# A two-layer transformer trunk on one core: reciprocal roots in three steps, spread by four column products

## The chip, the core and the metric

The kernel runs on one core of a Trainium2 chip. The metric is the device time of one execution in microseconds (us). Before the change three runs gave 1095.64, 1095.83 and 1101.1 us, median 1095.83. The engines are named as in the profile: PE is TensorE (matrix products; PEld is its loading of the stationary operand), DVE is VectorE, ACT is ScalarE, POOL is GpSimd, and SP issues the DMA transfers.

## What is computed

The reference runs two layers over 512 tokens of 1024 channels. Layer 0 has attention (four global heads, four windowed heads, and 256 context tokens as extra keys), layer 1 a Fourier mixing with a linear map. Each layer ends with a gated feed-forward part of width 2816 with a depthwise convolution of three taps. Every sub-layer stands between two RMS norms:

```python
def rms_norm(x, g):
    xf = x.astype(F32)
    y = xf * lax.rsqrt(jnp.mean(xf * xf, axis=-1, keepdims=True) + EPS)
    return (y * g.astype(F32)).astype(x.dtype)
...
        x = x + g1 * rms_norm(y, norm_g[i, 1])
        h = modulate(rms_norm(x, norm_g[i, 2]), sh2, sc2)
        x = x + g2 * rms_norm(conv_ffn(h, ffn_w_up[i], ffn_conv_w[i], ffn_conv_b[i], ffn_w_down[i]), norm_g[i, 3])
```

So between any two large products there is a sum of squares over the 1024 channels, a reciprocal root for each token, and a multiplication of every channel of a token by that root.

## The kernel before

Channels lie on the 128 partitions in eight blocks, and the tokens along the free dimension, in two halves of 256 tokens. All large products are made as three products of split numbers (`mm3`, lines 107 to 110): a high part and a low part of each operand. The kernel is written with a scheduler that sets the order of the instructions on each engine from priorities (`later`), from dependences added by hand (`follow`, `in_turn`, `behind_pe`), and from its own estimate of when operands are ready. Each engine then runs its queue strictly in that order, so a place in PE's queue that is not yet ready holds up all products behind it.

A norm of 256 tokens goes through these steps:

- Sums: `stat_add` (line 211) multiplies the squares by a matrix of ones, a quarter of the tokens (64) at a time, into four strips of 32 partitions each. The sum of token quarter j stands on partitions 32j to 32j+31, in 64 columns.
- Root: `rstd` (lines 214 to 222) works on those 128x64 numbers. ACT makes a first value (line 217); DVE makes one Newton step in four instructions (lines 218 to 221), the first of which scales the sum and the others use ACT's value.
- Spread: `spread` (lines 240 to 251) brings all 256 roots to all partitions. DVE multiplies the 128x64 roots by a mask of 128x4 (line 242), which gives 128x256 numbers with only one partition in 32 kept per quarter; one product of 256 columns with a selecting matrix (line 247) sums over the partitions into PSUM; ACT copies the result to SBUF (line 250), unless `copy=False`.

`spread` is called 14 times: three times at the start (the `R` steps of `START`), four times around the first feed-forward part (`joined`, line 379), twice before the Fourier mixing (`gated`, line 419, and `spread_on`, line 429), twice at the way from the Fourier mixing into the second feed-forward part (`joint`, line 460, for token half 0 and half 1), twice in that part (lines 1559 and 1564), and once in `boundary` (line 370) near the end. In `joint` for half 0 there are also small products without use, `busy` (line 203), which keep PE running while it waits; the last two of them (line 471) read the masked roots. The spread of half 1 is tied behind an update of half 0 (`after=self.mark`, line 463).

The squares of an output block are added up by `YStat.add` (lines 296 to 321): POOL adds the blocks 1 to 6 into an accumulator (line 318), and the last block is summed on PE with the accumulator.

At the very end of the program (lines 1913 to 1921) the last norm does not use `rstd` and `spread`. `stat_all` (line 225) multiplies by a whole 128x128 matrix of ones, so that the sums of 256 tokens are at once on all partitions, and `rstd_all` (line 228) makes the root there on 128x256 numbers: two ACT and three DVE instructions. Then DVE multiplies and adds, two channel blocks at a time, and four DMAs write the output.

Of the kernel before, what the change touches and what calls it, by code (L numbers as in the profile page):

```python
# [19 lines left out]
P = 128  # L20
# [61 lines left out]
K_ID, K_SEL, K_QD, K_ALL = 0, 128, 256, 260  # L82
# [3 lines left out]
def kernel(ctx: ExitStack, tc: tile.TileContext, a):  # L86
# [116 lines left out]
    def busy(ps, src, n):  # L203
        for _ in range(n):
            PE.matmul(ps[:32, :src.shape[1]], lhsT=ones32, rhs=src, start=True, stop=True)
# [8 lines left out]
    def rstd(ps):  # L214
        w = ps.shape[1]
        v, t, r = (mk(cp, [P, W4], F32, "st_" + c, n)[:, :w] for c, n in (("v", 2), ("t", 1), ("r", 1)))
        S.activation(out=r, in_=ps, func=AF.Abs_reciprocal_sqrt, bias=eps, scale=1.0 / D)
        V.tensor_scalar(out=v, in0=ps, scalar1=1.0 / D, scalar2=EPS, op0=ALU.mult, op1=ALU.add)
        V.tensor_tensor(out=t, in0=r, in1=r, op=ALU.mult)
        V.scalar_tensor_tensor(out=t, in0=t, scalar=-0.5, in1=v, op0=ALU.mult, op1=ALU.mult)  # L220
        V.scalar_tensor_tensor(out=v, in0=t, scalar=1.5, in1=r, op0=ALU.add, op1=ALU.mult)
        return v


    def stat_all(ps, sq, first, last):
        PE.matmul(ps[:, :HT], lhsT=ones32[:, :1].to_broadcast([P, P]), rhs=sq, start=first, stop=last)

    def rstd_all(ps):
        ps = ps[:, :HT]
        r, t, v = (md() for _ in range(3))  # L230
        R = mk(cp, [P, HT], F32, "Rs", 3)
        S.activation(out=r, in_=ps, func=AF.Abs_reciprocal_sqrt, bias=eps, scale=1.0 / D)
        S.activation(out=v, in_=ps, func=AF.Identity, bias=eps, scale=1.0 / D)
        V.tensor_tensor(out=t, in0=r, in1=r, op=ALU.mult)
        V.scalar_tensor_tensor(out=t, in0=t, scalar=-0.5, in1=v, op0=ALU.mult, op1=ALU.mult)
        V.scalar_tensor_tensor(out=R, in0=t, scalar=1.5, in1=r, op0=ALU.add, op1=ALU.mult)
        return R


    def spread(r, pps, tag="misc", copy=True, after=None):  # L240
        Rs = mk(cp, [P, HT], F32, "Rs", 3)
        i = V.tensor_tensor(out=Rs.rearrange("p (j w) -> p j w", j=4), in0=r.unsqueeze(1).to_broadcast([P, 4, W4]),
                            in1=con[:, K_QD:K_QD + 4].unsqueeze(2).to_broadcast([P, 4, W4]), op=ALU.mult)
        if after is not None:
            follow(i, after)
        R = mk(pps, [P, T], F32, tag, 2)
        PE.matmul(R[:, :HT], lhsT=con[:, K_SEL:K_SEL + P], rhs=Rs, start=True, stop=True)
        if not copy:
            return R[:, :HT], Rs
        S.copy(out=Rs, in_=R[:, :HT])  # L250
        return Rs
# [33 lines left out]
    class YStat:  # L285

        def __init__(self, pool=None, direct=1, late=None):
            self.pool = pool
            self.late = late
            self.direct = direct  # L290
            self.acc = None
            self.n = [0, 0]
            self.ps = {}
            self.last = {0: [], 1: []}

        def add(self, pps, src, hs):
# [7 lines left out]
            if n == 0:  # L304
                S.activation(out=self.acc[:, sl], in_=src, func=AF.Square)
                return
            if self.late and hs == [1] and n >= KC - 3:
                sq = mk(self.late, [P, T], F32, "cv%d" % (n % 2), 2)
                S.activation(out=sq[:, sl], in_=src, func=AF.Square)
                self.last[1].append(sq)  # L310
                return
# [10 lines left out]

        def sums_all(self, pps, h):
            ps = mk(pps, [P, T], F32, "misc", 2)
            stat_all(ps, self.acc[:, halves[h]], True, False)
            stat_all(ps, self.last[h][0][:, halves[h]], False, True)
            return ps
# [89 lines left out]
    class Plain:  # L417
# [11 lines left out]
        def spread_on(self, r, pps):  # L429
            Rp, _ = spread(r, pps, copy=False)  # L430
            R = mk(cp, [P, HT], F32, "Rs", 3)
            S.copy(out=R, in_=Rp)
            self.h, self.R = 1, (Rp, R)
# [26 lines left out]
        def joint(self, ys, h, pps, am):  # L460
            hs = halves[h]
            if h:
                R = spread(rstd(ys.sums(pps, h)[:, :W4]), pps, after=self.mark)
            else:
                ps = ys.sums(pps, h)
                warm = mk(pps, [P, T], F32, "mm", 6)
                for s, n in zip(halves, HOT2):
                    busy(warm, ys.sq[:, s], n)
                with later(-10000):
                    R, Rs = spread(rstd(ps[:, :W4]), pps, copy=False)  # L470
                busy(warm, Rs, HOT2[2])
                self.ps = mk(pps, [P, T], F32, "mm", 6)
# [22 lines left out]
            else:  # L495
# [7 lines left out]
                self.mark = i[2][1]  # L503
# [915 lines left out]
    def ffn(l, xp, ready, pre, mid, gem, plain=None):  # L1419
        nonlocal xT  # L1420
        ys = YStat(late=xp.pool if l == 0 else None)
# [482 lines left out]
    with ExitStack() as es:  # L1904
# [11 lines left out]
        R = rstd_all(ys.sums_all(pps, 1))  # L1916
        for k in range(0, KC, 2):
            t = mk(cp, [P, T], F32, "sq", 2).rearrange("p (a b) -> p a b", a=2)
            V.tensor_tensor(out=t, in0=yT[:, k:k + 2, hb], in1=R.unsqueeze(1).to_broadcast([P, 2, HT]), op=ALU.mult)
# [4 lines left out]
def _constants():  # L1924
    con = np.zeros((P, K_ALL), np.float32)
    con[:, K_ID:K_ID + P] = np.eye(P)
    con[::32, K_SEL:K_SEL + P] = 1.0
# [88 lines left out]
```

## Time and profile before

| what | value |
|---|---|
| median of three runs | 1095.83 us |
| the profiled execution | 1097.22 us |
| its span, first to last instruction | 1095.4 us |
| time around the span | 1.8 us |
| PE busy, share of the span | 1068.3 us, 98% |
| DVE busy | 891.7 us, 81% |
| ACT busy | 600.4 us, 55% |
| POOL busy | 113.0 us, 10% |
| mean granted PE clock | 0.996 |

The profile has one row for each group of instructions of one line on one engine. A row of the timeline gives the start, the duration, the engine, the line, the operation, what it writes from what, the shape, the count and, in brackets, the idle time of the engine before it with the instruction that ended it. A row of the chain of waits gives the start, the time that the chain spent there, and the engine with the line. Products are pipelined: the start of one is where it enters, and its duration holds the way through the array, so the time that a product takes from others is read from start to start. The four-byte products that are not split (the spreads, the sums) appear as two records each, with a weight load for each record.

### The profile page before, as it was taken

To read this page: it belongs to the slowest core of one execution; us is meant where nothing else is said; L and a number is where in the kernel's file an instruction comes from. 1 tells how busy PE (TensorE), PEld (TensorE's weight loads), DVE (VectorE), ACT (ScalarE), POOL (GpSimd) and SP (SyncE) were. 2 spreads that over 40 slices of the span, in tenths; PEclk is the share of its full clock that TensorE was granted. 3 is DMA by queue.
4 is the path that set the end of the run, shared out by engine and by line. 5 is a ranking of instruction groups with operands and counts; after the bars stand their busy time and mean duration, and the time that the engine had idled before them with its cause. 6 is when DMAs were issued, how large, how long until landed. Compare 5 with 4: busy or idle time off the path is not lost.

```text
span 1095.4 us, 22485 instructions
## 1 busy us (share of the span) xinstructions
PE 1068.3 (98%) x9340; PEld 1008.1 (92%) x9340; DVE 891.7 (81%) x1450; ACT 600.4 (55%) x1055; POOL 113.0 (10%) x121
## 2 busy tenths in 40 slices
PE   9999999999999999999999999999999999999995
PEld 5699888879999999999999999979999999999995
DVE  5779877773679976978999777888997899889856
ACT  4442366675666633652465466767755465556533
POOL 0046122422100000000000010210000000000012
PEclk9999999999999999999999999999999999999998
DMA  9776100174231564336724610842205533322332
GB/s 367 283 259 212 39 3 37 65 275 162 78 155 39 174 250 163 146 101 246 255 92 150 233 53 21 254 131 117 96 30 161 206 106 115 113 90 99 118 143 78
DMA packets 33911, 156.53 MB, mean 143 GB/s; under 512 B 3472, under 2 KB 8208, under 8 KB 22160
## 3 DMA queue, kind: packets, MB, share of 16 engines
q1 hardware_dynamic: 32656, 150.89, 38.2%
q0 software_dynamic: 1152, 4.19, 1.7%
q8 instruction: 73, 1.20, 0.4%
q14 instruction: 30, 0.25, 0.1%
HBM read 148.78 MB, written 6.29 MB: 142 GB/s over the span
## 4 chain that ended last, share of the span: by engine, by line
PE 75%; DVE 13%; ACT 5%; DMA 4%; issue 2%; POOL 0%; DVEq 0%; POOLq 0%; SPq 0%; ACTq 0%
PE mm L108 20%; PE mm L110 20%; PE mm L109 20%; DVE wl L144 3%; PE PT L1112 1%; ACT wh L144 1%; PE gm L108 1%; DVE gacc L566 1%; DVE cv L1443 1%; DVE cv L1445 1%; PE gm L109 1%; PE gm L110 1%; ACT yT L365 1%; PE O L109 1%; PE S L108 1%
## 5 line engine op out<-in xcount | busy, mean ns | idle before, releaser
L144 ACT CAST wh<-raw 128x1024 fp32r<-128x1024 f32 (+2 forms) x206 | 190.0, 931 | 150.0 <-PE mm L109 103.2
L144 DVE TENSOR_TENSOR wl<-raw,wh 128x1024 fp32r<-128x1024 f32 (+2 forms) x206 | 220.2, 1075 | 24.9 <-ACT wh L144 24.8
L108 PE MATMUL mm<-hh,wh 128*128 128x256 f32 x856 | 238.7, 280 | 1.1 <-ACT sq L1381 0.8
L110 PE MATMUL mm<-hh,wl 128*128 128x256 f32 x856 | 237.5, 278 | 1.2 <-DVE wl L144 1.0
L109 PE MATMUL mm<-hl,wh 128*128 128x256 f32 x856 | 237.9, 278 | 0.4 <-DVE hl L368 0.3
L108 PEld LDWEIGHTS mm<-hh,wh 128*128 128x128 f32 x856 | 160.6, 188 | 3.4 <-ACT sq L1381 1.2
L110 PEld LDWEIGHTS mm<-hh,wl 128*128 128x128 f32 x856 | 160.6, 188 | 2.2 <-DVE wl L144 2.1
L109 PEld LDWEIGHTS mm<-hl,wh 128*128 128x128 f32 x856 | 161.5, 189 | 0.8 <-DVE hl L368 0.5
L108 PE MATMUL mm<-xh,wh 128*128 128x256 f32 x492 | 137.0, 279 | 0.0
L109 PE MATMUL mm<-xl,wh 128*128 128x256 f32 x492 | 136.7, 278 | 0.0
L110 PE MATMUL mm<-xh,wl 128*128 128x256 f32 x492 | 136.5, 278 | 0.0
L108 PE MATMUL mm<-zh,wh 128*128 128x256 f32 x384 | 107.1, 279 | 0.3
L109 PE MATMUL mm<-zl,wh 128*128 128x256 f32 x384 | 106.7, 278 | 0.0
L110 PE MATMUL mm<-zh,wl 128*128 128x256 f32 x384 | 106.7, 278 | 0.0
L108 PEld LDWEIGHTS mm<-xh,wh 128*128 128x128 f32 x492 | 92.4, 188 | 1.3 <-ACT yT L1472 0.4
L109 PEld LDWEIGHTS mm<-xl,wh 128*128 128x128 f32 x492 | 92.5, 188 | 0.6 <-issue 0.4
L110 PEld LDWEIGHTS mm<-xh,wl 128*128 128x128 f32 x492 | 92.4, 188 | 0.1
L108 PEld LDWEIGHTS mm<-zh,wh 128*128 128x128 f32 x384 | 72.2, 188 | 1.0 <-ACT sq L1379 0.9
L109 PEld LDWEIGHTS mm<-zl,wh 128*128 128x128 f32 x384 | 72.4, 189 | 0.0
L110 PEld LDWEIGHTS mm<-zh,wl 128*128 128x128 f32 x384 | 72.1, 188 | 0.0
L318 POOL TENSOR_TENSOR gacc<-gacc,sq 128x256 f32<-128x256 f32 (+1 forms) x23 | 20.3, 881 | 387.7 <-ACT sq L316 387.3
L1442 ACT ACTIVATE cv<-mm,cols 128x512 f32<-128x512 f32 x59 | 45.6, 775 | 12.6 <-DVE mm L1386 6.8
(464 smaller groups left out, 2777.7 us busy)
## 6 DMA issues: line engine op xcount, KB each, us to landing
raw<-in_w_up SPq DMA_DIRECT2D x42, 1024.0 KB, 4.9
xT<-in_mod_r SPq DMA_DIRECT2D x20, 1024.0 KB, 5.1
raw<-in_w_down SPq DMA_DIRECT2D x32, 384.0 KB, 3.1
raw<-in_mod_p SPq DMA_DIRECT2D x8, 1024.0 KB, 4.9
raw<-in_w_down SPq DMA_DIRECT2D x16, 512.0 KB, 4.5
raw<-in_w_in SPq DMA_DIRECT2D x6, 1024.0 KB, 8.3
yT<-in_mod_r SPq DMA_DIRECT2D x10, 512.0 KB, 6.4
raw<-in_w_out SPq DMA_DIRECT2D x4, 1024.0 KB, 5.8
```

The lines of the kernel that those rows point to most:

```text
L108: i = PE.matmul(out, lhsT=ah, rhs=bh, start=start, stop=False, skip_group_check=skip)
L109: PE.matmul(out, lhsT=ah, rhs=bl, start=False, stop=False, skip_group_check=skip)
L110: return i, PE.matmul(out, lhsT=al, rhs=bh, start=False, stop=stop, skip_group_check=skip)
L144: i = S.copy(out=h, in_=src), eng.tensor_tensor(out=l, in0=src, in1=f(h), op=ALU.subtract)
L318: G.tensor_tensor(out=self.acc[:, sl], in0=self.acc[:, sl], in1=sq[:, sl], op=ALU.add)
L365: S.activation(out=yT[:, c, halves[h]], in_=yT[:, c, halves[h]], func=AF.Identity, bias=bm[:, c:c + 1], scale=am[:, c:c + 1])
L566: held(V.scalar_tensor_tensor(out=acc, in0=w[:, i, :], scalar=scol[:, 0, k:k + 1], in1=acc, op0=ALU.mult, op1=ALU.add))
L1112: PE.transpose(out=pt[:, j * P:(j + 1) * P], in_=Ps[j][:, off:off + P], identity=ident)
L1442: S.activation(out=cv, in_=ps, func=AF.Identity, bias=bc, scale=wc[1])
L1443: V.scalar_tensor_tensor(out=cv[:, 1:], in0=ps[:, :T - 1], scalar=wc[0], in1=cv[:, 1:], op0=ALU.mult, op1=ALU.add)
L1445: V.scalar_tensor_tensor(out=cv[:, :T - 1], in0=ps[:, 1:], scalar=wc[2], in1=cv[:, :T - 1], op0=ALU.mult, op1=ALU.add)
```

## The change

Three things are changed in the code.

- `rstd` has three DVE instructions: t = r * (-0.5/D) * r, t = (sum + D*EPS) * t, and root = (t + 1.5) * r. The second reads the sum from PSUM.
- `spread` has no DVE instruction. It makes four products of 64 columns each. Product j takes one column of the 128x4 mask, repeated 128 times, as the stationary operand, and the 128x64 roots as the moving one; its result is the token quarter j on all partitions. The `busy` products in `joint` read the roots, and the tie `after=self.mark` is gone.
- The last norm uses `rstd` and `spread`. Its first multiplication reads PSUM and the others a copy in SBUF. The squares of the last two blocks of that norm are summed on PE (`tail=2` in layer 1), instead of the last alone, by `stat_add` instead of `stat_all`.

```diff
+K_ID, K_PAD, K_QD, K_ALL = 0, 128, 256, 260
...
         S.activation(out=r, in_=ps, func=AF.Abs_reciprocal_sqrt, bias=eps, scale=1.0 / D)
-        V.tensor_scalar(out=v, in0=ps, scalar1=1.0 / D, scalar2=EPS, op0=ALU.mult, op1=ALU.add)
-        V.tensor_tensor(out=t, in0=r, in1=r, op=ALU.mult)
-        V.scalar_tensor_tensor(out=t, in0=t, scalar=-0.5, in1=v, op0=ALU.mult, op1=ALU.mult)
+        V.scalar_tensor_tensor(out=t, in0=r, scalar=-0.5 / D, in1=r, op0=ALU.mult, op1=ALU.mult)
+        V.scalar_tensor_tensor(out=t, in0=ps, scalar=D * EPS, in1=t, op0=ALU.add, op1=ALU.mult)
         V.scalar_tensor_tensor(out=v, in0=t, scalar=1.5, in1=r, op0=ALU.add, op1=ALU.mult)
...
-    def spread(r, pps, tag="misc", copy=True, after=None):
+    def spread(r, pps, tag="misc", copy=True):
+        R = mk(pps, [P, T], F32, tag, 2)
+        for j in range(4):
+            PE.matmul(R[:, j * W4:(j + 1) * W4], lhsT=con[:, K_QD + j:K_QD + j + 1].to_broadcast([P, P]), rhs=r,
+                      start=True, stop=True)
+        if not copy:
+            return R[:, :HT]
         Rs = mk(cp, [P, HT], F32, "Rs", 3)
-        i = V.tensor_tensor(out=Rs.rearrange("p (j w) -> p j w", j=4), in0=r.unsqueeze(1).to_broadcast([P, 4, W4]),
-                            in1=con[:, K_QD:K_QD + 4].unsqueeze(2).to_broadcast([P, 4, W4]), op=ALU.mult)
-        if after is not None:
-            follow(i, after)
-        R = mk(pps, [P, T], F32, tag, 2)
-        PE.matmul(R[:, :HT], lhsT=con[:, K_SEL:K_SEL + P], rhs=Rs, start=True, stop=True)
-        if not copy:
-            return R[:, :HT], Rs
         S.copy(out=Rs, in_=R[:, :HT])
...
+            if hs == [1] and n >= KC - self.tail:
+                sq = mk(cp, [P, T], F32, "sq", 2)
+                S.activation(out=sq[:, sl], in_=src, func=AF.Square)
+                self.last[1].append(sq)
+                return
...
-                R = spread(rstd(ys.sums(pps, h)[:, :W4]), pps, after=self.mark)
+                R = spread(rstd(ys.sums(pps, h)[:, :W4]), pps)
...
-                    R, Rs = spread(rstd(ps[:, :W4]), pps, copy=False)
-                busy(warm, Rs, HOT2[2])
+                    r = rstd(ps[:, :W4])
+                    R = spread(r, pps, copy=False)
+                for _ in range(HOT2[2]):
+                    PE.matmul(warm[:32, :HT], lhsT=ones32, rhs=r.unsqueeze(1).to_broadcast([P, 4, W4]), start=True,
+                              stop=True)
...
-        ys = YStat(late=xp.pool if l == 0 else None)
+        ys = YStat(late=xp.pool if l == 0 else None, tail=2 * l)
...
-        R = rstd_all(ys.sums_all(pps, 1))
+        Rp = spread(rstd(ys.sums(pps, 1)[:, :W4]), pps, copy=False)
+        R = mk(cp, [P, HT], F32, "Rs", 3)
+        S.copy(out=R, in_=Rp)
...
-            V.tensor_tensor(out=t, in0=yT[:, k:k + 2, hb], in1=R.unsqueeze(1).to_broadcast([P, 2, HT]), op=ALU.mult)
+            V.tensor_tensor(out=t, in0=yT[:, k:k + 2, hb], in1=both(R if k else Rp), op=ALU.mult)
```

The functions `stat_all`, `rstd_all` and `sums_all` are removed.

The scheduler sets the order anew. In the rows below a line number is that of the file the row belongs to, and the number behind a name is that of the buffer; in the changed file `rstd` is on lines 217 to 220, the four products of `spread` on line 227 and its copy on line 232.

On DVE, before the Fourier mixing (`gated`; Rs is the masked or the copied root, st_v the root, wl the low part of a weight), there stands before:

```order
L218 TENSOR_SCALAR st_v_7708<-misc_7699 128x64
L219 TENSOR_TENSOR st_t_7709<-st_r_7710 128x64
L220 SCALAR_TENSOR_TENSOR st_t_7709<-st_t_7709,st_v_7708 128x64
L1468 TENSOR_TENSOR yT_68<-yT_68,mm_7753 128x256
L221 SCALAR_TENSOR_TENSOR st_v_7708<-st_t_7709,st_r_7710 128x64
L144 TENSOR_TENSOR wl_7690<-mm_7691,wh_7689 128x512
L144 TENSOR_TENSOR wl_7690<-mm_7695,wh_7689 128x512
L242 TENSOR_TENSOR Rs_7716<-st_v_7708,con_66 128x256
```

In the changed kernel the same place on DVE reads:

```order
L218 SCALAR_TENSOR_TENSOR st_t_7716<-st_r_7717 128x64
L219 SCALAR_TENSOR_TENSOR st_t_7716<-misc_7706,st_t_7716 128x64
L220 SCALAR_TENSOR_TENSOR st_v_7715<-st_t_7716,st_r_7717 128x64
L1452 TENSOR_TENSOR yT_68<-yT_68,mm_7761 128x256
L144 TENSOR_TENSOR wl_7697<-mm_7698,wh_7696 128x512
L144 TENSOR_TENSOR wl_7697<-mm_7702,wh_7696 128x512
```

The root no longer has three other instructions between its steps and the spread. On PE the spread of the same place moves with it: it stood behind 20 products of its PSUM tile, and now it stands behind 3 of them, 17 places earlier. At the other four places where the scheduler moves it, it stands 3 to 6 products earlier.

On DVE, at the way from the Fourier mixing into the second feed-forward part (`joint`; the first group of st_ rows is half 0, the second half 1; misc is PSUM), there stands before:

```order
L221 SCALAR_TENSOR_TENSOR st_v_8866<-st_t_8867,st_r_8868 128x64
L242 TENSOR_TENSOR Rs_8874<-st_v_8866,con_66 128x256
L218 TENSOR_SCALAR st_v_9090<-misc_8848 128x64
L219 TENSOR_TENSOR st_t_9091<-st_r_9092 128x64
L220 SCALAR_TENSOR_TENSOR st_t_9091<-st_t_9091,st_v_9090 128x64
L221 SCALAR_TENSOR_TENSOR st_v_9090<-st_t_9091,st_r_9092 128x64
L480 TENSOR_TENSOR md_t_8881<-yT_68,misc_8876 128x256
L481 TENSOR_TENSOR xT_67<-xT_67,md_t_8881 128x256
```

In the changed kernel the same place on DVE reads:

```order
L220 SCALAR_TENSOR_TENSOR st_v_8872<-st_t_8873,st_r_8874 128x64
L218 SCALAR_TENSOR_TENSOR st_t_9097<-st_r_9098 128x64
L219 SCALAR_TENSOR_TENSOR st_t_9097<-misc_8854,st_t_9097 128x64
L465 TENSOR_TENSOR md_t_8887<-yT_68,misc_8879 128x256
L220 SCALAR_TENSOR_TENSOR st_v_9096<-st_t_9097,st_r_9098 128x64
L466 TENSOR_TENSOR xT_67<-xT_67,md_t_8887 128x256
```

The last step of half 1's root has moved between the multiplication (line 465) and the addition (line 466) of half 0. On PE, three of half 1's four spread products now stand ahead of the first sweep of the feed-forward part and one inside it, where the whole spread stood before.

On PE, at the end of the program (gacc is POOL's accumulator), there stands before:

```order
L108 MATMUL mm_13323<-xh_12625,wh_13113 128x256
L109 MATMUL mm_13323<-xl_12626,wh_13113 128x256
L110 MATMUL mm_13323<-xh_12625,wl_13114 128x256
L226 MATMUL misc_13353<-gacc_12957,ones_7_70 128x256
L226 MATMUL misc_13353<-sq_13343,ones_7_70 128x256
```

In the changed kernel the same place on PE reads:

```order
L109 MATMUL mm_13332<-xl_12635,wh_13122 128x256
L110 MATMUL mm_13332<-xh_12634,wl_13123 128x256
L211 MATMUL misc_13362<-gacc_12966,ones_7_70 32x64 x4
L211 MATMUL misc_13362<-sq_13330,ones_7_70 32x64 x4
L211 MATMUL misc_13362<-sq_13352,ones_7_70 32x64 x4
L227 MATMUL misc_13382<-st_v_13375,con_66 128x64 x4
```

Two products of 256 columns have become twelve of 64 columns on strips of 32 partitions, and the spread comes behind them. On POOL one addition of line 318 is gone. The order of the DMA issues on SP is the same row by row.

More of the change, by code (lines that the diff above doesn't have):

```diff
@@ L80 @@
 C_SINK, C_ALL = 528, 532
-K_ID, K_SEL, K_QD, K_ALL = 0, 128, 256, 260
+K_ID, K_PAD, K_QD, K_ALL = 0, 128, 256, 260
 @with_exitstack
@@ L217, in rstd @@
         S.activation(out=r, in_=ps, func=AF.Abs_reciprocal_sqrt, bias=eps, scale=1.0 / D)
-        V.tensor_scalar(out=v, in0=ps, scalar1=1.0 / D, scalar2=EPS, op0=ALU.mult, op1=ALU.add)
-        V.tensor_tensor(out=t, in0=r, in1=r, op=ALU.mult)
-        V.scalar_tensor_tensor(out=t, in0=t, scalar=-0.5, in1=v, op0=ALU.mult, op1=ALU.mult)
+        V.scalar_tensor_tensor(out=t, in0=r, scalar=-0.5 / D, in1=r, op0=ALU.mult, op1=ALU.mult)
+        V.scalar_tensor_tensor(out=t, in0=ps, scalar=D * EPS, in1=t, op0=ALU.add, op1=ALU.mult)
         V.scalar_tensor_tensor(out=v, in0=t, scalar=1.5, in1=r, op0=ALU.add, op1=ALU.mult)
         return v
[L225 to L237, printed above, removed]
-    def spread(r, pps, tag="misc", copy=True, after=None):
-        Rs = mk(cp, [P, HT], F32, "Rs", 3)
-        i = V.tensor_tensor(out=Rs.rearrange("p (j w) -> p j w", j=4), in0=r.unsqueeze(1).to_broadcast([P, 4, W4]),
-                            in1=con[:, K_QD:K_QD + 4].unsqueeze(2).to_broadcast([P, 4, W4]), op=ALU.mult)
-        if after is not None:
-            follow(i, after)
-        R = mk(pps, [P, T], F32, tag, 2)
-        PE.matmul(R[:, :HT], lhsT=con[:, K_SEL:K_SEL + P], rhs=Rs, start=True, stop=True)
-        if not copy:
-            return R[:, :HT], Rs
+    def spread(r, pps, tag="misc", copy=True):
[5 more added lines that the diff above has]
+            return R[:, :HT]
+        Rs = mk(cp, [P, HT], F32, "Rs", 3)
         S.copy(out=Rs, in_=R[:, :HT])
@@ L285, with __init__ @@
     class YStat:
-        def __init__(self, pool=None, direct=1, late=None):
+        def __init__(self, pool=None, direct=1, late=None, tail=0):
+            self.tail = tail
             self.pool = pool
@@ L321, in add @@
                 self.last[h].append(sq)
[L323 to L327, printed above, removed]
         def sums(self, pps, h):
@@ L429, in spread_on @@
         def spread_on(self, r, pps):
-            Rp, _ = spread(r, pps, copy=False)
+            Rp = spread(r, pps, copy=False)
             R = mk(cp, [P, HT], F32, "Rs", 3)
@@ L502, in joint @@
                     follow(turn[n], turn[n - 1])
-                self.mark = i[2][1]
             yield
@@ L1926, in _constants @@
     con[:, K_ID:K_ID + P] = np.eye(P)
-    con[::32, K_SEL:K_SEL + P] = 1.0
     con[np.arange(0, P, 32), K_QD + np.arange(4)] = 1.0
```

## The prediction

> **What bounds the kernel now.** I read the page first: the busy time of the engines and the chain of work that ended last. Both name PE.
>
> ```profile
> PE 1068.3 (98%) x9340; PEld 1008.1 (92%) x9340; DVE 891.7 (81%) x1450; ACT 600.4 (55%) x1055; POOL 113.0 (10%) x121
> PE 75%; DVE 13%; ACT 5%; DMA 4%; issue 2%; POOL 0%; DVEq 0%; POOLq 0%; SPq 0%; ACTq 0%
> ```
>
> PE has 27 us of the 1095.4 us span without work. So the change can gain only where PE waits for a root, at the start and at the end, and whatever it adds to PE's work counts almost everywhere. Next I read, in the timeline, one norm from the root to the copy, in the middle of the output projection.
>
> ```profile
> 274.68 0.31 ACT L217 ACTIVATE st_r<-misc,con 128x64 f32<-128x64 f32 x1 [0.67 <-PE misc L211]
> 275.02 0.23 DVE L218 TENSOR_SCALAR st_v<-misc 128x64 f32<-128x64 f32 x1 [8.65 <-ACT st_r L217]
> 275.17 0.21 DVE L219 TENSOR_TENSOR st_t<-st_r 128x64 f32<-128x64 f32 x1
> 275.42 0.22 DVE L220 SCALAR_TENSOR_TENSOR st_t<-st_t,st_v 128x64 f32<-128x64 f32 x1
> 275.67 0.22 DVE L221 SCALAR_TENSOR_TENSOR st_v<-st_t,st_r 128x64 f32<-128x64 f32 x1
> 275.93 0.42 DVE L242 TENSOR_TENSOR Rs<-st_v,con 128x256 f32<-128x256 f32 x1
> ...
> 276.25 0.28 PE L110 MATMUL mm<-hh,wl 128*128 128x256 f32 x1
> 276.50 0.67 PE L247 MATMUL misc<-Rs,con 128*128 128x256 f32 x2
> 277.21 0.37 ACT L250 COPY Rs<-misc 128x256 f32<-128x256 f32 x1 [2.22 <-PE misc L247]
> ```
>
> Line 218 doesn't use ACT's value, yet it starts only after ACT's end at 274.99, so it lies on the path. The next step starts 0.15 us later, the others 0.25 to 0.26 after each other; the mask ends at 276.35, and PE begins 0.15 later.
>
> **The change part by part.** *The root.* Without lines 218 and 242 the value is ready earlier by 0.15 (275.02 to 275.17) and by 0.42 plus the gap ahead of it, 0.02 to 0.04: 0.59 us in all. From ACT's end to the value it takes 0.03 + 0.25 + 0.26 + 0.22 = 0.76. I assume that the step which now reads PSUM costs what line 218, reading PSUM too, cost (0.23).
>
> *The spread on PE.* What it costs now, where it doesn't wait, and what its weight loads cost, stands in the timeline of PE, in the line's own rows (least, median and greatest duration in ns) and in the timeline of the loads:
>
> ```profile
> 756.98 0.28 PE L110 MATMUL mm<-hh,wl 128*128 128x256 f32 x1
> 757.10 0.60 PE L247 MATMUL misc<-Rs,con 128*128 128x256 f32 x2
> ...
> 757.65 0.28 PE L109 MATMUL mm<-hl,xh 128*128 128x256 f32 x1
> ```
>
> ```profile
> L247 PEld LDWEIGHTS misc<-Rs,con x28: 185/188/191, 11.8 to 1071.8; 128*128 128x128 f32 x28
> L247 PE MATMUL misc<-Rs,con x28: 377/379/484, 11.8 to 1072.0; 128*128 128x256 f32 x28
> ```
>
> ```profile
> 756.98 0.30 PEld L247 LDWEIGHTS misc<-Rs,con 128*128 128x128 f32 x2
> ...
> 682.92 0.20 PEld L512 LDWEIGHTS misc<-con,st_v 128*64 128x64 f32 x4
> ```
>
> From 756.98 to 757.65 stand one product before, the spread and one after: 0.67 less two of 0.12 is 0.43 us. The two records begin 0.60 - 0.38 = 0.22 apart (379 ns is the median of one), so a pass takes 0.22 for 256 columns, and 0.054 for 64. After the change there are four products of two records, eight passes: 0.43 us of columns again. But each record loads a stationary operand 128 columns wide. The two loads at 756.98 are 0.19 long (188 ns) and end 0.30 after the first began, so the second began 0.11 later. Line 512 has four loads 64 wide, two for each half of the array, which end 0.20 after the first began, although only 2 columns move: the load's time goes by the columns loaded, whatever moves. Eight loads take 8 x 0.107 = 0.86 us. A load can run behind the pass ahead of it, but that is only 0.054 long. I take 0.86 and not 0.43, since line 512 is the nearest row: 0.43 more for each spread that PE runs without a wait, and 0.11 more where the first load isn't hidden (0.97).
>
> The Trainium skill, "TensorE: Matmul & The Clock Gate", section "Back-to-back issue gap", gives about 81 ns for each load and product in a stream of 128 columns, which speaks for less. By it eight would take an estimated 0.65, the surplus would be half of mine, and the sum below about +0.7 us in place of +2.5. No row here has a 128-wide load with 64 moving columns.
>
> *Spreads that PE doesn't wait for.* The chain of waits runs through three of them:
>
> ```profile
> 312.17 0.44 PE misc L247 x2
> ...
> 668.42 0.43 PE misc L247 x2
> ...
> 751.71 0.45 PE misc L247 x2
> 752.17 0.37 ACT Rs L250
> ...
> 759.00 0.26 ACT Rs L250
> ```
>
> Here the earlier value gains nothing, since the spread's place on PE comes later anyway: +0.4 each, 1.2 us. The fourth, at 757.10, ends by 757.8 while its copy starts only with ACT at 759.00: 0. The third one at the start, near 36 us, has neither row: between 0 and 0.43, I take 0.2.
>
> *Spreads that PE waits for.* Five have moved ahead in PE's queue, by 5, 3, 6, 17 and 5 products of 0.114 (290.49 to 290.60 below), since the scheduler expects the value earlier.
>
> ```profile
> 290.49 0.28 PE L109 MATMUL mm<-hl,xh 128*128 128x256 f32 x1
> 290.60 0.28 PE L110 MATMUL mm<-hh,xl 128*128 128x256 f32 x1
> 291.18 0.70 PE L247 MATMUL misc<-Rs,con 128*128 128x256 f32 x2 [0.30 <-DVE Rs L242]
> ...
> 645.90 0.28 PE L109 MATMUL mm<-xl,wh 128*128 128x256 f32 x1
> 646.47 0.67 PE L247 MATMUL misc<-Rs,con 128*128 128x256 f32 x2 [0.29 <-DVE Rs L242]
> ...
> 1071.01 0.28 PE L108 MATMUL mm<-xh,wh 128*128 128x256 f32 x1
> 1071.65 0.70 PE L247 MATMUL misc<-Rs,con 128*128 128x256 f32 x2 [0.36 <-DVE Rs L242]
> ```
>
> At 276: the place was free at 276.37, PE began at 276.50, and the cost was 0.13 + 0.54 = 0.67. Now the place is 0.57 earlier, 275.80, and the value comes 0.59 earlier: a wait of 0.1 and 0.97, so +0.4. At 291: place 290.72, begun 291.18, cost 1.0; now place 290.38, value for 290.59, cost 0.21 + 0.97, so +0.2. At 301 (six places, a short wait): between 0 and +0.43, I take +0.2. At 646: place 646.02, cost 0.45 + 0.54 = 0.99; now place 644.08. The value there was behind two instructions of line 144, which now come after it; ACT's root ended at 643.34,
>
> ```profile
> 643.02 0.32 ACT st_r L217
> ...
> 1070.75 0.85 DVE Rs L242
> ```
>
> so PE can begin at 643.34 + 0.76 + 0.15 = 644.25: a wait of 0.17 and 0.97, +0.2. At 1071 the mask took 0.85, beside POOL; without it the value is 1.03 earlier, at 1070.62, for the place at 1070.56: 0.06 + 0.97 against 1.06, 0. Together +1.0 us.
>
> *The start.* The chain there, in pieces:
>
> ```profile
> 11.83 0.64 PE misc L247 x2
> 12.49 0.38 ACT Rs L250
> ...
> 19.87 0.67 PE misc L247 x2
> ```
>
> The first spread stands behind other products until 11.83, so its value isn't waited for; the copy and the warm-up products behind it come 0.37 to 0.43 later: +0.4. The second gains its wait, at most 0.26, and loses 0.43: +0.15.
>
> *`joint`.* DVE is the path here: mask, then half 1's four steps, then the first update.
>
> ```profile
> 724.75 0.42 DVE Rs L242
> ...
> 726.03 0.43 DVE md_t L480
> ```
>
> Now PE begins at 724.75 + 0.15; from begin to use it takes the 0.71 of 276.50 to 277.21 plus 0.43: the update starts at 726.04, as before. One step of half 1, 0.26, now stands between the update's two instructions, so the sweep starts up to 0.3 later. Against that, three quarters of half 1's spread run while PE waits, and a spread of 0.43 inside the sweep becomes 0.21. I take 0, between -0.4 and +0.3.
>
> *The end.* POOL's last addition and the last square end together, at 1083.70 and 1083.77:
>
> ```profile
> 1080.53 3.17 POOL L318 TENSOR_TENSOR gacc<-gacc,sq 128x256 f32<-128x256 f32 x4 [0.38 <-ACT sq L316]
> ...
> 1083.35 0.42 ACT L316 ACTIVATE sq<-yT 128x256 f32<-128x256 f32 x1
> ...
> 1087.02 1.29 DVE L1919 TENSOR_TENSOR sq<-yT,Rs 128x512 f32<-128x512 f32 x2
> ```
>
> So `tail` gains nothing alone. The chain becomes: 0.45 from the square to ACT's root (an estimate: a record's 379 ns and two beginnings of about 0.03), 0.31 for it, 0.76 + 0.15 to PE, 0.71 + 0.43 to the use: 1083.77 + 2.81 = 1086.58 against 1087.02. The gain is 0.4; what follows, multiplications, additions and stores, moves with it. If POOL's addition had stayed, nothing would be later than this, so it has no price.
>
> *The sum* against the profiled execution of 1097.22 us (1.8 above its span, 1.4 above the median): +0.55 start, +0.2 third spread, +1.0 waited for, +1.2 not waited for, 0 `joint`, -0.4 end: +2.55, I say +2.5, or 1099.7. On the median of 1095.83 that is **1098.3 us**. About 0.5%, 5.5 us, is what a measurement of this kernel can tell from no change, so this reads as no change.
>
> **The rivals.** *The loads are hidden.* If a load runs fully beside the passes, a spread keeps its 0.43, and only the waits change. Start -0.25, 291: 0.21 + 0.54 against 1.0, -0.25; 301 -0.2; 646 0.17 + 0.54 against 0.99, -0.3; 1071 0.06 + 0.54 against 1.06, -0.45; `joint` -0.4; end -0.8. That is -2.65, or 1093.2. For it speaks that loads of 128 columns vanish behind products of 256 all through the kernel; against it, line 512. By the Trainium skill, same page, section "Step-by-step: what each phase is for", loads are pulled ahead of running products, which would bring this about if more than one could be ahead.
>
> *It does nothing.* The chain isn't on PE for 25% of the span, and behind a spread other waits may swallow 0.4 us: only the end's 0.4 would stay, 1095.4.
>
> *Slower: the place outruns the value.* PE's queue is strict, and the five spreads have moved up by 36 products, 4.1 us. If the values come no earlier than the masks did, because DVE is held by other work when ACT's root is ready, PE waits those 4.1 us and pays five times 0.43 besides: 6.25 in place of 1.0, a sum of +7.8, or 1103.6. It decides from the point where the values are 0.6 late at all five places (+3.0, past 0.5%). For it speaks that PE waited for the masks there (0.30, 0.29 and 0.36 in the brackets above); against it, that at 275.02 DVE had itself waited 8.65 for ACT.
>
> **How the numbers follow.** Forecast 0.45, with a range of its own of 1096.6 to 1100; loads hidden 0.25; nothing 0.2; slower 0.1. The range of 8 in 10 goes from below the hidden loads, 1092.8, to between the forecast and the slower rival, 1101.2. Only half a per cent counts: faster 0.03 (twice the gain of the hidden loads), slower 0.09 (the last rival), no difference 0.88.
>
> **What would show it.** In the profile after, the loads of line 227 should lie 0.107 apart, and a spread not waited for should cost 0.86 (products on both sides); 0.43 would mean hidden loads. The root should come 0.76 after ACT. The first multiplication of the last norm should start 2.8 after the last square. Waits of PE at the five places above 0.5 would be the slower rival. The prediction is wrong if the median leaves the range, and its reason is wrong if the loads lie closer than 0.08.

## The result and the profile after

The changed kernel takes 1102.12 us, median of ten runs (1100.48 to 1105.47); the kernel before takes 1096.09 us beside it (ten runs, 1093.89 to 1101.1). The ratio is 1.0051, 95% interval 1.0037 to 1.0065: 5.5 to 6 us slower, just above the range on record (1092.8 to 1101.2). The profiled executions differ by less: spans of 1095.4 and 1099.9 us, +4.5.

The page of the changed kernel, busy time by engine:

```profile
PE 1073.4 (98%) x9452; PEld 1015.5 (92%) x9452; DVE 882.8 (80%) x1420; ACT 600.3 (55%) x1055; POOL 112.5 (10%) x120
```

DVE lost 8.9 us of work and PE gained 5.1. PE was the bound at 98% before and is so now.

A spread that PE doesn't wait for, in the timeline (start, duration, engine; the spread that stood at 757.10 before):

```profile
760.59 0.28 PE L110 MATMUL mm<-hh,wl 128*128 128x256 f32 x1
760.59 0.97 PEld L227 LDWEIGHTS misc<-st_v,con 128*128 128x128 f32 x8
760.71 1.00 PE L227 MATMUL misc<-st_v,con 128*128 128x64 f32 x8
...
761.72 0.28 PE L109 MATMUL mm<-hl,xh 128*128 128x256 f32 x1
```

From the product before to the product that comes second after the spread are 1.13 us; less two products of 0.117 that is 0.90, where it was 0.43. Eight loads fill 0.97 us: the last is 0.19 long, so they begin 0.78 / 7 = 0.111 apart. This is the mechanism that the prediction took, at its size (0.107 and 0.86).

A place that PE waits for, six products earlier in PE's queue than before:

```profile
300.75 1.29 DVE L350 TENSOR_TENSOR hl<-yT,hh 128x512 fp32r<-128x512 f32 x2 [2.20 <-ACT hh L349]
...
301.14 0.31 ACT L217 ACTIVATE st_r<-misc,con 128x64 f32<-128x64 f32 x1
...
301.96 0.22 DVE L218 SCALAR_TENSOR_TENSOR st_t<-st_r 128x64 f32<-128x64 f32 x1
...
302.29 0.22 DVE L219 SCALAR_TENSOR_TENSOR st_t<-misc,st_t 128x64 f32<-128x64 f32 x1
...
302.49 0.28 PE L109 MATMUL mm<-hl,wh 128*128 128x256 f32 x1
302.55 0.22 DVE L220 SCALAR_TENSOR_TENSOR st_v<-st_t,st_r 128x64 f32<-128x64 f32 x1
302.92 1.07 PE L227 MATMUL misc<-st_v,con 128*128 128x64 f32 x8
...
304.01 0.28 PE L108 MATMUL mm<-hh,xh 128*128 128x256 f32 x1
```

ACT's value is there at 301.45, but DVE works on another subtraction until 302.04, so the root comes 1.32 after ACT and not 0.76. PE, free at 302.60, begins at 302.92: a wait of 0.3. From 302.49 to 304.01 are 1.52 us, less two products 1.29 for wait and spread. The step that reads PSUM (line 219) starts 0.33 after the step ahead of it; steps that read SBUF start 0.26 after.

The end, from the last square to the first multiplication:

```profile
1087.36 0.42 ACT L292 ACTIVATE sq<-yT 128x256 f32<-128x256 f32 x1 [0.93 <-DVE yT L1452]
...
1088.22 0.31 ACT L217 ACTIVATE st_r<-misc,con 128x64 f32<-128x64 f32 x1
...
1089.16 0.23 DVE L220 SCALAR_TENSOR_TENSOR st_v<-st_t,st_r 128x64 f32<-128x64 f32 x1
...
1089.53 1.49 PE L227 MATMUL misc<-st_v,con 128*128 128x64 f32 x8 [1.38 <-DVE st_v L220]
1091.06 0.37 ACT L1902 COPY Rs<-misc 128x256 f32<-128x256 f32 x1 [2.53 <-PE misc L227]
1091.54 0.69 DVE L1905 TENSOR_TENSOR sq<-yT,misc 128x512 f32<-128x512 f32 x1 [2.15 <-ACT Rs L1902]
```

The square ends at 1087.78 and the multiplication starts at 1091.54: 3.76, where 2.81 was forecast and 3.25 stood before. The spread alone takes 1.53 from its first product to its copy. The windows of this stretch (length, busy time of PE, PEld, DVE, ACT and POOL with counts, then the granted PE clock, the share of the DMA engines and GB/s) show why it is that long:

```profile
1089.50:1090.10 0.60, 0.57 (x5) 0.60 (x6) 0.00 (x0) 0.00 (x0) 0.00 (x0) 0.93 0.00 0
1090.10:1091.10 1.00, 0.93 (x5) 0.74 (x4) 0.00 (x0) 0.04 (x1) 0.00 (x0) 0.50 0.00 0
```

Half-way through the spread the clock falls to 0.50, after PE had stood still for 1.38 us ahead of it (the bracket of the spread's row).

### The profile page after: what moved, and what is told of

It is laid out like the page before. It is cut to its first block, busy times and chain, and to the rows that moved or that the text cites. A ratio compares the mean times of both kernels' runs of the same rounds, so it can differ in the third digit from the quotient of the medians.

```text
span 1099.9 us, 22696 instructions
## 1 busy us (share of the span) xinstructions
PE 1073.4 (98%) x9452; PEld 1015.5 (92%) x9452; DVE 882.8 (80%) x1420; ACT 600.3 (55%) x1055; POOL 112.5 (10%) x120
## 4 chain that ended last, share of the span: by engine, by line
PE 74%; DVE 13%; ACT 6%; DMA 4%; issue 3%; POOL 0%; DVEq 0%; SPq 0%; ACTq 0%; POOLq 0%
PE mm L108 20%; PE mm L110 19%; PE mm L109 19%; DVE wl L144 3%; PE PT L1096 1%; PE misc L227 1%; ACT wh L144 1%; ACT yT L347 1%; DVE cv L1427 1%; DMA xl<-in_mod_r 1%; DVE cv L1429 1%; DVE gacc L550 1%; PE gm L108 1%; PE O L109 1%; PE gm L109 1%
```

## The experiments

The theory: eight weight loads of 128 columns, 0.11 us each, make a spread cost 0.90 in place of 0.44, and this is the loss. The rivals: the earlier places in PE's queue, the root, or the end.

**The masked spread put back.**

```diff
-        for j in range(4):
-            PE.matmul(R[:, j * W4:(j + 1) * W4], lhsT=con[:, K_QD + j:K_QD + j + 1].to_broadcast([P, P]), rhs=r, ...)
+        V.tensor_tensor(out=Rs..., in0=r..., in1=con[:, K_QD:K_QD + 4]..., op=ALU.mult)
+        PE.matmul(R[:, :HT], lhsT=con[:, K_SEL:K_SEL + P], rhs=Rs, start=True, stop=True)
```

> The changed kernel with the masked spread of before (one DVE mask, one product of 256 columns), the three-step root and the new end kept. Theory (the eight 128-wide weight loads of a spread hold PE, 0.45 us more at nearly every one of the 14 places): about 5 us of the 6 come back, median about 1096.5 (ratio to before 1.000 to 1.002, since the new end stays), and a spread that isn't waited for costs 0.44 again. Rival (the earlier places in PE's queue, the root or the end are what costs): the time stays above 1099 (ratio above 1.003).

Measured: 1097.09 us, ratio 1.0005 (0.9985 to 1.0025). The loss is gone with nothing but the spread undone. The spread that stood at 751 before, which PE doesn't wait for either:

```profile
753.60 0.28 PE L110 MATMUL mm<-hh,wl 128*128 128x256 f32 x1
753.72 0.59 PE L229 MATMUL misc<-Rs,con 128*128 128x256 f32 x2
...
754.26 0.28 PE L109 MATMUL mm<-hl,xh 128*128 128x256 f32 x1
```

0.66 less two products is 0.43. The root and the end fall as rivals, since both are still the new ones here. The earlier places don't fall by this run: with the mask back, the five spreads that had moved stand within two products of where they stood before. The strips, further down, decide on them.

**Only the root.** The three lines of `rstd` in the kernel before.

```diff
-        V.tensor_scalar(out=v, in0=ps, scalar1=1.0 / D, scalar2=EPS, op0=ALU.mult, op1=ALU.add)
-        V.tensor_tensor(out=t, in0=r, in1=r, op=ALU.mult)
-        V.scalar_tensor_tensor(out=t, in0=t, scalar=-0.5, in1=v, op0=ALU.mult, op1=ALU.mult)
+        V.scalar_tensor_tensor(out=t, in0=r, scalar=-0.5 / D, in1=r, op0=ALU.mult, op1=ALU.mult)
+        V.scalar_tensor_tensor(out=t, in0=ps, scalar=D * EPS, in1=t, op0=ALU.add, op1=ALU.mult)
```

> The kernel before with only the three-step root. Theory: the value comes 0.15 us earlier at the few spreads that PE waits for and nothing else moves: ratio 0.999 to 1.000. Rival (the step that reads PSUM is slow, or the root in three steps disturbs DVE's order): above 1.001.

Measured: 1096.53 us, 0.9999 (0.9982 to 1.0017). The root neither gains nor loses anything that can be measured.

**Only the four products**, in the kernel before.

> The kernel before with only the four-product spread (four-step root, old end). Theory: the spread alone brings most of the loss, ratio 1.004 to 1.005, and the unwaited spreads cost 0.90. Rival (the spread is no more than a third of the loss): below 1.002.

Measured: 1103.14 us, 1.0065 (1.0043 to 1.0088), above what the theory gave. The timeline showed something else beside the loads: two records of the second half's spread in `joint` stand at 743.13, 14 us behind the other six (at 728.78).

```profile
743.13 0.43 PE L243 MATMUL misc<-st_v,con 128*128 128x64 f32 x2
...
744.01 1.29 DVE L481 TENSOR_TENSOR md_t<-yT,Rs 128x512 f32<-128x512 f32 x2
```

The copy and the updates wait for the last quarter, and then PE for the updates (waits of PE, 735 to 760 us):

```profile
PE mm L108 <- ACT hh L484: 2.9, 1, 2.9
```

One product had become four, which the scheduler may place apart. So the same again with that spread kept together:

```diff
-                R = spread(rstd(ys.sums(pps, h)[:, :W4]), pps)
+                r = rstd(ys.sums(pps, h)[:, :W4])
+                with later(-10000):
+                    R = spread(r, pps)
```

> The fourth experiment (the kernel before with only the four-product spread), with the second half's spread of the step from the Fourier mixing to the feed-forward part kept together in PE's queue, so that none of its products stands late. Theory (each of the spreads loses 0.45, less where PE waited anyway, and the end is as before): 0.45 x 10 to 12 less some 0.5 of shorter waits, +3.5 to +4.5 us on before, ratio 1.003 to 1.0045, and no wait of PE above 2 us between 735 and 760. Rival (the fourth experiment's loss was that late spread alone): ratio 1.001 or less.

Measured: 1100.0 us, 1.0033 (1.0014 to 1.0051), without a wait of PE between 735 and 760. The products alone cost about 3.6 us; the late quarter had cost some 3 us more. In the changed kernel that quarter stands at 733.70, and PE has no such wait. The changed kernel's 6.0 lie 2.4 above these 3.6; the two intervals overlap, so no run says what the 2.4 are, or whether they are more than chance.

**Twice as many loads**, for as many moved columns.

```diff
-        for j in range(4):
+        w = W4 // 2
+        for j in range(8):
+            PE.matmul(R[:, j * w:(j + 1) * w], lhsT=con[:, K_QD + j // 2:K_QD + j // 2 + 1].to_broadcast([P, P]),
+                      rhs=r[:, j % 2 * w:j % 2 * w + w], start=True, stop=True)
```

> The changed kernel with each of the four products cut in two: eight products of 32 columns each, so 16 weight loads of 128 columns where there were 8, and the same number of moved columns. Theory (loads set the price, 0.11 each): an unwaited spread costs 0.90 + 8 x 0.112 = 1.8 us, and with some 12 spreads on the path the time is about 10 us longer than the changed kernel's, ratio to before 1.012 to 1.016. Rival (moved columns or the places set the price): 0.9 a spread, ratio 1.005. In the last spread, which comes after PE had stood still, the loads are 0.11 apart at first and 0.21 after some 0.4 us, as in the changed kernel.

Measured: 1111.81 us, 1.0141 (1.0111 to 1.0172), 9.7 us above the changed kernel. The spread of 751 again:

```profile
763.50 0.28 PE L110 MATMUL mm<-hh,wl 128*128 128x256 f32 x1
763.62 1.86 PE L228 MATMUL misc<-st_v,con 128*128 128x32 f32 x16
...
765.52 0.28 PE L109 MATMUL mm<-hl,xh 128*128 128x256 f32 x1
```

2.02 less 0.23 is 1.79, or 0.112 for each load. The price goes by the loads of full width, whatever moves. In the last spread the loads lay 0.11 apart at first and 0.21 from the ninth on, where the clock was at 0.50.

**Narrower loads.** Each product in four strips of 32 partitions.

```diff
         for j in range(4):
-            PE.matmul(R[:, j * W4:(j + 1) * W4], lhsT=con[:, K_QD + j:K_QD + j + 1].to_broadcast([P, P]), rhs=r, ...)
+            for g in range(0, P, 32):
+                PE.matmul(R[g:g + 32, j * W4:(j + 1) * W4], lhsT=con[...].to_broadcast([P, 32]), rhs=r, ...)
```

> The changed kernel with each of the four products cut into four strips of 32 partitions, so that a spread has 16 products and 32 weight loads, but each load is 32 columns wide. Theory, if the width of a load sets its price (the sums of squares, line 211, have such loads, 8 of them in about 0.14 us): a spread takes 0.45 to 0.60, ratio 1.000 to 1.002. Rival, if each load costs 0.107 whatever its width: 3.4 us a spread, ratio above 1.02. If the spread's price had no part in the loss: as the changed kernel, 1.005.

Measured: 1102.48 us, 1.0049 (1.0028 to 1.007). As a time that speaks for the third reading, that the spread's price had no part. But the second half's spread in `joint` had again come apart: 10 of its 32 records stood at 728, 12 at 732 and 10 at 746, and against the changed kernel 5.4 us were lost between 747 and 756: PE waited 3.0 us, and behind the wait its clock stood at 0.50 for 3.4 us (last section). With that spread kept together:

> The strips of the third experiment, with the second half's spread of the step from the Fourier mixing to the feed-forward part given the priority that the first half's has, so that its 16 products stand together in PE's queue. Theory (5.4 us of the third experiment's time came from products of that one spread that stood 15 us late in the queue): that wait is gone, and with unwaited spreads of 0.67 the time lies between before and the changed kernel, ratio 1.001 to 1.004. Rival (the strips themselves cost as much as four full products): 1.005 again.

Measured: 1096.51 us, 1.0001 (0.9983 to 1.0019). The timeline of PE at the unwaited spread that stood at 312 before:

```profile
312.39 0.28 PE L110 MATMUL mm<-hh,wl 128*128 128x256 f32 x1
312.60 0.65 PE L228 MATMUL misc<-st_v,con 128*32 128x64 f32 x32
...
313.40 0.28 PE L109 MATMUL mm<-hl,xh 128*128 128x256 f32 x1
```

1.01 less two products is 0.78: more than the 0.45 to 0.60 expected, but far from 3.4, with 32 loads where there were 8. So it isn't the number of loads that counts: 32 narrow ones on four strips take less time than 8 of full width. Whether it is their width, or that the loads of four strips run beside each other, this run doesn't separate. The records themselves begin within 0.44 (312.60 to 313.03), and 0.34 lies ahead of them and behind them, where PE goes from full width to strips and back. The whole is level with before, better than the theory gave: in this program the new end takes 2.93 from the last square to the first multiplication, and the start is 0.24 shorter than in the first profile of before. The five spreads that had moved stand here within one product of their places in the changed kernel, so the earlier places alone cost nothing that can be measured: that rival falls here.

**The end of before**, in the changed kernel.

> The changed kernel with the end of before (sums with a whole matrix of ones, root on 128x256 numbers, one square on TensorE). One look at the end alone. Theory (the last spread, at 1.5 us from its first product to its copy, made the new end longer): from the last square to the first multiplication 3.25 us as before, against 3.76 in the changed kernel; the unwaited spreads stay at 0.90. Rival (the end is longer since the last square comes later): 3.7 or more here too.

```profile
1087.42 0.70 PE L225 MATMUL misc<-gacc,ones 128*128 128x256 f32 x2
1087.96 0.42 ACT L319 ACTIVATE sq<-yT 128x256 f32<-128x256 f32 x1 [0.93 <-DVE yT L1473]
...
1088.43 0.70 PE L225 MATMUL misc<-sq,ones 128*128 128x256 f32 x2 [0.32 <-ACT sq L319]
...
1091.27 1.29 DVE L1924 TENSOR_TENSOR sq<-yT,Rs 128x512 f32<-128x512 f32 x2
```

From 1088.38 to 1091.27 are 2.89, not the 3.25 expected: POOL's accumulator is ready before the last square here, where it came as late as the square in the first profile of before. The new end is longer than this by 0.4 to 0.9 (3.33 and 3.76, below).

**PE kept running at the end**, by four products without use.

> The changed kernel with four products without use of 256 columns on PE at the end, two before the last sums and two between them and the last spread, so that PE hardly stands still. One look at the end alone. Theory (the load spacing of 0.21 us in the last spread is a slower clock that follows PE's standing still): all loads of the last spread are 0.11 apart, the spread takes 1.1 to 1.2 us to its copy in place of 1.53, and the first multiplication comes 0.3 to 0.4 us earlier after the last square (3.4 in place of 3.76). Rival (the spacing belongs to the end for another reason, as another engine's traffic): 0.21 again, 3.7.

```profile
1094.03 1.07 PE L227 MATMUL misc<-st_v,con 128*128 128x64 f32 x8 [0.54 <-DVE st_v L220]
```

The spread is short and the way 3.33, as the theory said. But the next run takes the proof away.

**Both kernels once more.**

> The kernel before once more, for a second profile of the same program. Theory (the two cadences of the 256-column products, 0.113 and 0.118 us, belong to the execution and not to the program): some stretch that had one of them in the first profile has the other here (812 to 885 us was at 0.118), and the last square is followed by the first multiplication after 2.9 us and not 3.25, since POOL's last addition is only sometimes the later one. Rival (they belong to the program): the same stretches at the same cadence within 2 us.

> The changed kernel once more, for a second profile of the same program. Theory: unwaited spreads cost 0.90 again and the end takes 3.76 from the last square to the first multiplication again, while the stretches at 0.118 differ (884 to 930 us was at 0.118, 820 to 865 at 0.113). Rival (they belong to the program): the same stretches again.

The changed kernel's end in its second profile:

```profile
1088.30 0.42 ACT L292 ACTIVATE sq<-yT 128x256 f32<-128x256 f32 x1 [0.93 <-DVE yT L1452]
...
1090.47 1.07 PE L227 MATMUL misc<-st_v,con 128*128 128x64 f32 x8 [1.38 <-DVE st_v L220]
1091.58 0.37 ACT L1902 COPY Rs<-misc 128x256 f32<-128x256 f32 x1 [2.11 <-PE misc L227]
1092.05 0.69 DVE L1905 TENSOR_TENSOR sq<-yT,misc 128x512 f32<-128x512 f32 x1 [1.73 <-ACT Rs L1902]
```

3.33 without any added product, so the expected 3.76 was wrong. The clock falls to 0.50 in this execution too, but at 1092.5, a microsecond behind the spread, where in the first profile it fell at 1090.0, inside it. So when it falls differs from one execution to the next, and the added products are not shown to have kept it up. The kernel before has its 3.25 again, where 2.9 was expected:

```profile
1080.24 0.42 ACT L316 ACTIVATE sq<-yT 128x256 f32<-128x256 f32 x1
1080.64 0.30 PEld L226 LDWEIGHTS misc<-gacc,ones 128*128 128x128 f32 x2 [1.16 <-POOL gacc L318]
...
1083.91 1.29 DVE L1919 TENSOR_TENSOR sq<-yT,Rs 128x512 f32<-128x512 f32 x2
```

In five profiles of before (three more follow) it is 3.25 three times and 2.89 twice: POOL's addition is late in some executions. What these two profiles say of the cadences stands in the last section.

**Both forms, each where it is cheaper.** Masked where PE doesn't wait (the last spread of `joined`, `spread_on`, and the two in the second feed-forward part), strips elsewhere.

> The three-step root everywhere, the strips where PE waits for the value and at the two ends, the masked spread at the four places where PE doesn't wait, the new end. Theory (a masked spread costs 0.44 there and strips 0.67; where PE waits, the mask's time is saved): 4 x 0.23 us less than the strips everywhere, about 1 us less than before, ratio 0.998 to 1.000. Rival (the switch between the two forms costs more than it saves): above 1.001.

Measured: 1096.15 us, 0.9997 (0.9978 to 1.0015). No version here is measurably faster than the kernel before.

**A wait near 515.** The spreads and the end add to some 3.5 us (the table below), and the medians are 6.0 apart. Comparing the waits of PE from 505 to 525 us showed one more, in the changed kernel:

```profile
PE misc L588 <- DVE gacc L550: 1.2, 1, 1.2
```

DVE's sum waits there for a 1 MB transfer of modulation weights, which the change doesn't touch:

```profile
506.93 1.28 DVE L550 SCALAR_TENSOR_TENSOR gacc<-xT,cols,gacc 128x1024 f32<-128x1024 f32 x1 [2.03 <-DMA xT<-in_mod_r]
```

The same in the first profile of before:

```profile
503.00 1.28 DVE L566 SCALAR_TENSOR_TENSOR gacc<-xT,cols,gacc 128x1024 f32<-128x1024 f32 x1 [0.99 <-DMA xT<-in_mod_r]
```

Four profiles have the changed kernel's program up to there (both of its own, and those with the old and the warmed end): PE waits 1.2, 0.7, 2.4 and 3.2 us, 1.9 in the mean. Two of before had 0.2 and 0. Whether that is the program or chance:

> The kernel before, a third profile. Theory (the wait of PE near 515 us for the sum behind the 1 MB transfer comes with the changed kernel): at most 0.6 us here. Rival (it comes by chance in any execution, as its sizes 0.7, 1.2, 2.4 and 3.2 in one program suggest): among this and the next three profiles at least one has 1 us or more.

> The kernel before, a fourth profile, for the same question. Theory: at most 0.6 us near 515. Rival: 1 us or more in some of the four.

> The kernel before, a fifth profile, for the same question. Theory: at most 0.6 us near 515. Rival: 1 us or more in some of the four.

> The changed kernel with the masked spread, a second profile. Theory (the wait near 515 comes with the four products): at most 0.6 us, as in its first profile. Rival: 1 us or more in some of the four.

Measured: no wait of PE for that sum in any of the four; DVE waited 0.5 to 0.8 for the transfer, and the times were 1094.1, 1096.3, 1098.08 and 1094.46 us. So with five profiles at 0 to 0.2 against four at 0.7 to 3.2 the wait comes with the changed kernel, about +1.8. It doesn't come with the loads as such: the strips and the eight products have none, the four products in the kernel before have 0.5 and 1.8, and the mixed kernel has 2.9. Why the transfer lands later isn't shown.

The same comparison at 627 goes the other way. PE waits there for a copy of ACT, which stands behind a cast that waits for a transfer of weights (`in_w_down`); in the first profile of before and in that of the changed kernel:

```profile
PE misc L614 <- ACT gacc L607: 1.2, 1, 1.2
```

```profile
PE misc L598 <- ACT gacc L591: 0.3, 1, 0.3
```

In the five profiles of before this wait is 1.2, 1.0, 0, 0 and 1.0 us, in the four with the changed kernel's program 0.3 and three times 0: about -0.6. A part of what is lost at 515 thus comes back here.

## Why the prediction missed

The mechanism was right. The loads of line 227 lie 0.111 apart (0.107 said), an unwaited spread costs 0.90 (0.86 said), and doubling the loads doubles it. The sum was too small. The table compares the spacing of the same split products on both sides of each place, after against before, in the first pair of profiles and in the second pair; changes inside a stream of such products (the cadence, below) and other waits that come and go between profiles of one program are left out. The values are read to about 0.1.

| term | forecast | first pair | second pair |
|---|---|---|---|
| start, two spreads | +0.55 | +0.44 | +0.72 |
| third spread of the start | +0.2 | 0 | 0 |
| the four at 276 to 312 | +1.2 | +1.37 | +1.37 |
| 646, 668 | +0.6 | +0.75 | +0.69 |
| `joint` | 0 | +0.23 | +0.23 |
| 751 | +0.4 | +0.45 | +0.46 |
| 757, with a wait at 764 that goes | 0 | -0.23 | -0.25 |
| 1071 | 0 | +0.15 | +0.15 |
| the end | -0.4 | +0.49 | +0.07 |
| sum of the forecast's terms | +2.55 | +3.65 | +3.44 |
| the wait near 515 | none | +1.02 | +0.65 |
| the wait at 627 | none | -0.85 | -1.22 |

- *The wait near 515* is the term that the prediction didn't have, 1.8 us in the mean of nine profiles. It would have needed the question which transfers land just in time and what a shift does to them. The same question gives the wait at 627, -0.6 in the same profiles. With both the terms make 4.6 to 4.9 of the 6.0 us between the medians. Pair by pair they explain less: 3.8 of the 4.5 us between the spans of the first pair, and 2.9 of 8.2 in the second.
- *The end* was wrong in a wait. The text took 0.71 + 0.43 from the spread's first product to its use, since the first multiplication reads PSUM. In `joint`, where nothing is copied, this is what the changed kernel takes, 1.14:

```profile
727.58 1.10 PE L227 MATMUL misc<-st_v,con 128*128 128x64 f32 x8
...
728.72 0.42 DVE L465 TENSOR_TENSOR md_t<-yT,misc 128x256 f32<-128x256 f32 x1 [0.31 <-PE misc L227]
```

  At the end ACT copies the same values, and the multiplication starts 0.10 after that copy has ended (1092.05 against 1091.95 in the second profile), 1.58 after the first product; its bracket names the copy. A place of before that also reads PSUM beside a copy showed it already:

```profile
669.19 0.37 ACT L432 COPY Rs<-misc 128x256 f32<-128x256 f32 x1
...
669.59 0.69 DVE L438 TENSOR_TENSOR md_t<-yT,misc 128x512 f32<-128x512 f32 x1 [0.36 <-ACT Rs L432]
```

  Why a multiplication waits for a copy that it doesn't read isn't shown. The root's value, too, came 0.86 after ACT (1088.53 to 1089.39) and not 0.76. With 0.44 and 0.1 more, 2.81 becomes the 3.3 of the second profile; in the first the halved clock put 0.43 on top. So a gain of 0.4 became a loss.
- *The waited-for places* came out near their sum, with another working: the value was assumed 0.59 earlier, but at 302 DVE was busy until 302.04, and it came 1.32 after ACT. PE's wait there was 0.3, and between 0.1 and 0.5 at the five places, below the 0.6 from which the slower rival decides; and the strips have the early places and the time of before. The slower rival didn't happen.
- *The spread at 757* was set at nothing since its copy starts later anyway. That reason was wrong: PE pays 0.46 whoever waits for the copy. The value held because PE had waited for DVE behind it, and this wait is gone after:

```profile
765.01 0.39 PE L109 MATMUL mm<-hl,wh 128*128 128x256 f32 x1 [0.33 <-DVE hl L368]
```

- *Loads hidden* fell by 0.111. The Trainium skill, "TensorE: Matmul & The Clock Gate", section "Back-to-back issue gap", would give an estimated 0.65 for a spread; these rows give 0.90, so the measurement stands against it here. The same page, section "LDWEIGHTS (loading the stationary operand)", says that the load's time goes by the columns loaded, 128 / 1.2 = 107 ns; the rows agree (0.111).
- *It does nothing* fell: the unwaited spreads at 312, 668 and 751 each gave about 0.46, and only what stands at 757 was swallowed by another wait.

The failed steps are thus the end's term (-0.4 forecast, +0.07 and +0.49 measured, since the first multiplication waited for the copy) and the waits for transfers that were not in the sum (+1.8 near 515, -0.6 at 627); the range ended 0.9 us too low. Open stay the last 1.1 to 1.4 us (the interval, 1.0037 to 1.0065 of 1096, is 4.1 to 7.1 us) and what sets the landing of those transfers. The end alone was looked at and not timed.

## What to carry to other kernels

- Where PE is the bound, price an edit by what it puts into PE's queue, including a spread whose result nobody is waiting for; saved DVE work (8.9 us here) buys nothing. Then look for the wait behind it that may swallow the price, and for the transfers that land just in time, in both directions.
- Splitting a product by columns keeps the columns and multiplies the loads: 64 moved columns behind a 128-wide load cost 0.11 a record, not 0.054. Look at the loads of a narrow product before adding more of them, and narrow the load if the result allows.
- A reading of PSUM that stands beside a copy of the same values may wait for the copy. Look at what its row names as the releaser before you count on the shorter way.
- One product that becomes four can be placed apart by a scheduler; the last piece then sets the time. Compare the places of all pieces.

## What the runs showed of the hardware

The products of 256 columns run at two cadences at a granted clock of 1.00, and stay at one for tens of microseconds. The window of 820 to 865 us (products of PE in the first bracket) in the two profiles of before:

```profile
820.00:865.00 45.00, 45.00 (x384) 45.00 (x384) 37.42 (x50) 25.03 (x42) 0.00 (x0) 1.00 0.51 168
```

```profile
820.00:865.00 45.00, 45.00 (x400) 45.00 (x399) 39.05 (x50) 27.01 (x45) 0.00 (x0) 1.00 0.55 190
```

And in the two profiles of the changed kernel:

```profile
820.00:865.00 45.00, 45.00 (x400) 45.00 (x399) 38.80 (x52) 26.42 (x43) 0.00 (x0) 1.00 0.49 168
```

```profile
820.00:865.00 45.00, 45.00 (x384) 45.00 (x384) 38.16 (x50) 25.97 (x43) 0.00 (x0) 1.00 0.50 168
```

In 45 us 384 or 400 products, 0.117 or 0.1125 each, in either program: the cadence belongs to the execution, as was expected. What sets it is not known. Because of it, a comparison of two single profiles is blind to a few microseconds: the spans of the second pair are 8.2 apart (1092.3 and 1100.5), those of the first 4.5. The steps between neighbouring products inside the streams (those below 0.135 us) add up to 836.4 and 841.5 us in the two profiles of the changed kernel and to between 831.5 and 836.8 in the five of before: too few profiles to tell whether the change has a part in the cadence.

The granted clock falls to 0.50 at the end of all 18 profiles, when PE has little left to do, 1090.0 and 1092.5 us being the times in the changed kernel. In five of them it falls within the program as well, each time 0.6 to 2.0 us after the end of a wait of PE of 1.8 to 3.2 us, and stays there for 3.4 us: near 515 in the kernels with four products together, with both forms and with the warmed end, and near 750 in the two with a late piece of a spread. In the profile with the warmed end, after the wait of 3.2 us:

```profile
518.70:522.10 3.40, 3.40 (x18) 3.40 (x17) 2.02 (x3) 0.62 (x1) 0.00 (x0) 0.51 1.01 395
```

That is 18 products where 30 fit at 0.1125, some 1.4 us lost on top of the wait. Behind the wait of 2.4 us in the profile with the old end the clock didn't fall, so the length of a wait alone doesn't decide.

Four records with 32-wide loads on the four strips start 7 ns apart, and a round of four takes 0.055 us (the 32 records within 0.44), no longer than one pass of 64 columns: loads and passes of the strips run beside each other.
